# Folding two rows of a gate/up product in a matmul, fewer native down pieces and one more weight place

## The chip, the cores and the metric

The kernel runs on one core of one Trainium2 chip. The metric is the device time of one execution in microseconds (us); each timed value below is such an execution, and the median of them is compared. TensorE is called PE here, VectorE DVE, ScalarE ACT, GpSimd POOL and SyncE SP. Each engine runs its own instructions in the order in which the program's scheduler has put them; a weight load of PE (PEld) overlaps its matmuls.

## The reference

The program computes two blocks on 256 tokens of width 1024, all in float32. The first has adaptive normalisation, differential attention over 256 tokens and 256 context rows, a Fourier mixer, and a mixture of 32 experts of which each token takes two. The second has two layers of two feed-forward networks each, around a sparse attention and a gated mixer. What matters here is one expert:

```python
xb = h_pad[tok]                                          # rows of one expert
y = (jax.nn.silu(xb @ w_gate[e]) * (xb @ w_up[e])) @ w_down[e]
return y * wt[:, None]
```

`w_gate[e]` and `w_up[e]` are 1024 x 512, `w_down[e]` is 512 x 1024: 2 MiB each, 6 MiB an expert, 192 MiB for the 32 experts, all read from HBM once.

## The kernel before, in words

Weights stream in pieces of 1 MiB (128 partitions x 2048 float32). `load` (L59) issues the next piece on SP's queue into a place: five places belong to the pool `raw` (`RAW = 5`), and one more, `rawx`, is added from the end of the first block's mixer until the experts are done (`extend`, `NX = 1`). SP issues in stream order, and an issue waits until its place is free. For each expert the stream has four pieces of gate and up weights (g0, g1, u0, u1), and behind those of expert e the two down pieces of expert e-1 (d0, d1).

A split piece is cut into a high and a low part of the reduced float32 type that PE multiplies fastest: `split` (L151) rounds on ACT into `wh` (L152), and DVE subtracts into `wl` (L153). `ahead(3)` keeps up to three cut pieces in hand, in four buffers of each part; the place of a raw piece is free after its subtraction. A native piece is not cut: PE multiplies it as plain float32, and its place is free after those matmuls. `NATIVE` names (e mod 4, piece number); before, piece 5 (d1) is native in every expert.

One turn of the loop over e in `moe` does, in program order: `turn(e-1)`; the gate rows of e with g0 and g1 (`rows`); on every fourth e the one-hot selection of the next four experts (`hot`, DVE); two parts of `gather`; the up rows with u0 and u1; `place` (two transposes); `scatter(e-2)`; `down(e-1)` with d0 and d1. An expert has 64 places for tokens, and its stationary operand has 128 columns, 64 high parts and 64 low parts of the same tokens. So the product has two rows for each token, which must be added: `rows` copies the product from its PSUM bank to `gu0` or `gu1` (ACT, L1489), and `turn` transposes it on PE in four 128 x 128 pieces for gate and four for up (L1497); DVE adds the two rows in a reduction (`sum`, L1499). Then come silu (ACT, L1501), the product of gate and up (DVE, L1502) and its split into `act` (ACT and DVE, L152 and L153). `down` multiplies `act` with d0 and d1, and takes the result from PSUM scaled, as a high part on ACT (`yh`, L1520) and a low part on DVE (`yl`, L1521).

The order in which each engine does all this is laid down when the program is made, by a scheduler that puts ready instructions in by priority with durations of its own; so a piece's rounding on ACT can stand behind an instruction of another step that waits for PE, and then waits as well.

All matmuls go through `mm` (L143), so they have one line, L144; they are told apart by their tiles (moving operand first, then the stationary one).

Of the kernel before, what the change touches and what calls it, by code (L numbers as in the profile page):

```python
# [10 lines left out]
F32 = mybir.dt.float32  # L11
# [3 lines left out]
AF = mybir.ActivationFunctionType  # L15
OP = mybir.AluOpType
AX = mybir.AxisListType
PSUM = bass.MemoryType.PSUM
P = 128
# [1 line left out]
D = 1024  # L21
EPS = 1e-6
PIECE = 2048
RAW = 5
NX = 1
NEG = -1e30
SEL = -3e38
# [2 lines left out]
class Net:  # L30
    def __init__(self, ctx, tc, I, out):
        self.ctx, self.tc, self.nc, self.I, self.out = ctx, tc, tc.nc, I, out
        self.cp = self.pool(ctx, "const", 1)
        self.rawp = self.pool(ctx, "raw", RAW)
        self.psp = ctx.enter_context(tc.tile_pool(name="psum", bufs=4, space=PSUM))
# [8 lines left out]
        self.pieces = {}  # L44
        self.extra, self.extended, self.spare, self.slots_raw = {}, set(), 0, RAW
        self.parts = 1
# [43 lines left out]
    def extend(self, ctx, n):  # L90

        self.rawx = ctx.enter_context(self.tc.tile_pool(name="rawx", bufs=n, reuse_waits="tile", side="right"))
        self.spare, self.slots_raw = n, RAW + n
        self.run_loads()
# [1126 lines left out]
    def route_consts(self):  # L1221
        nc, I, cp = self.nc, self.I, self.cp
        self.idr = cp.tile([P, P], F32R, name="idr")
        nc.vector.tensor_copy(self.idr, self.idf)
        self.slots = cp.tile([P, P], F32, name="slots")
        nc.gpsimd.iota(self.slots, pattern=[[0, 2], [1, 64]], base=0, channel_multiplier=0,
                       allow_small_or_imprecise_dtypes=True)
        self.tri = cp.tile([P, P], F32, name="tri")
        nc.gpsimd.memset(self.tri, 1.0)
        nc.gpsimd.affine_select(out=self.tri, in_=self.tri, pattern=[[1, P]], compare_op=OP.is_gt, fill=0.0,  # L1230
                                base=0, channel_multiplier=-1)
        self.wr = cp.tile([P, 8, 36], F32, name="wr")
        nc.gpsimd.dma_start(self.wr[:, :, :4], I["w_router_group"][0].rearrange("(j p) e -> p j e", j=8))
        nc.gpsimd.dma_start(self.wr[:, :, 4:], I["w_router_expert"][0].rearrange("(j p) e -> p j e", j=8))
# [171 lines left out]
                            nc.vector.tensor_add(self.h[t][:, o], self.h[t][:, o], a)  # L1406


    NATIVE = ((0, 5), (1, 5), (2, 5), (3, 5))

    def native(self, e, n):

        return (e % 4, n) in self.NATIVE

# [15 lines left out]
    def moe(self):  # L1430
        nc, I = self.nc, self.I
        self.limit = self.moe_end
        with ExitStack() as ctx:
            mp = self.pool(ctx, "moe", 1)
            XG, G, GT, gu, act, ys, acc = {}, {}, {}, {}, {}, {}, {}
# [54 lines left out]
                gu[e, which] = sb  # L1490

            def turn(e):
                z = []
                for which in range(2):
                    ps = self.bank()
                    for a in range(4):
                        nc.tensor.transpose(ps[:, P * a : P * a + P], gu[e, which][:, P * a : P * a + P], self.idf)  # L1497
                    r = mp.tile([P, 4, 64], F32, name=f"sum{which}", bufs=1)
                    nc.vector.tensor_reduce(r, ps.rearrange("p (a i s) -> p a s i", a=4, i=2), axis=AX.X, op=OP.add)  # L1499
                    z.append(r)  # L1500
                nc.scalar.activation(z[0], z[0], AF.Silu)  # L1501
                nc.vector.tensor_mul(z[0], z[0], z[1])  # L1502
                A = mp.tile([P, 4, P], F32R, name="act", bufs=2)
                self.split(A[:, :, :64], A[:, :, 64:], z[0])
                act[e] = A

            def down(e):
# [33 lines left out]
            for e in range(34):  # L1541
                if e == 1:
                    self.parts = 1
                if 0 < e < 33:
                    turn(e - 1)
                if e < 32:
                    rows(e, 0)
                    if e % 4 == 0 and e < 28:
                        hot(e // 4 + 1)
                if e < 32:  # L1550
                    if e < 28:
                        for i in range(2):
                            gather(e // 4 + 1, 2 * (e % 4) + i)
                    rows(e, 1)
                    place(e)
                if e > 1:
                    scatter(e - 2)
                if 0 < e < 33:
                    down(e - 1)
# [105 lines left out]
```

## Time and profile before

| | before |
|---|---|
| median of 3 executions | 1911.88 us (1911.81 to 1913.43) |
| the profiled execution, own time | 1913.98 us |
| its span, first to last instruction | 1912.2 us |
| PE busy | 1837.8 us (96%) |
| DVE busy | 1327.7 us (69%) |
| ACT busy | 1146.4 us (60%) |
| POOL busy | 41.8 us (2%) |
| read from HBM | 447.92 MB, 235 GB/s over the span |

The experts take the stretch from about 226 to 800 us of the span. Busy time of PE is a union of modelled, pipelined matmuls: a PE that is busy all the time need not be at its peak. The DMA figure is the mean busy share of 16 DMA engines.

### The profile page before, as it was taken

What the parts mean: (1) busy time and instruction counts of PE and PEld (TensorE: products, weight loads), DVE (VectorE), ACT (ScalarE), POOL (GpSimd) and SP (SyncE); (2) the same over time, 40 slices, a digit from 0 to 9 for tenths busy, and PEclk for the clock granted to TensorE, in tenths of its full rate; (3) what the DMA queues carried; (4) which work ended last, traced back from release to release, by engine and by line L of the source; (5) the groups of instructions that cost most, each with busy time, mean ns of one, the idle gap of its engine ahead of it and who ended that gap; (6) DMA issues with size and microseconds to landing.
All of it is one profiled execution on the core that took longest, in us unless ns stands there. A gap on an engine that the chain in (4) does not pass through costs nothing.

```text
span 1912.2 us, 23030 instructions
## 1 busy us (share of the span) xinstructions
PE 1837.8 (96%) x8352; PEld 1439.9 (75%) x8352; DVE 1327.7 (69%) x2116; ACT 1146.4 (60%) x1924; POOL 41.8 (2%) x74
## 2 busy tenths in 40 slices
PE   6899699999999999999999999999999999999998
PEld 3677577766667666678888888887888888887886
DVE  2887788888888888865558765556555776765554
ACT  3555587778777777754456654446444755555443
POOL 2000000000000000000000000000000010100000
PEclk9999899999999999999999999999999999999999
DMA  9784398999999999865555455554555556665551
GB/s 301 257 284 144 111 340 356 349 357 353 351 357 352 353 365 367 277 220 177 179 179 178 155 176 198 198 186 153 190 198 198 182 172 198 199 218 191 181 180 43
DMA packets 189495, 450.51 MB, mean 236 GB/s; under 512 B 10170, under 2 KB 119066, under 8 KB 164802
## 3 DMA queue, kind: packets, MB, share of 16 engines
q1 hardware_dynamic: 185284, 437.26, 64.5%
q0 software_dynamic: 3808, 11.25, 2.1%
q8 instruction: 66, 1.08, 0.2%
q10 hardware_dynamic: 288, 0.52, 0.1%
q14 instruction: 49, 0.40, 0.1%
HBM read 447.92 MB, written 1.07 MB: 235 GB/s over the span
## 4 chain that ended last, share of the span: by engine, by line
PE 71%; DVE 8%; ACT 5%; issue 3%; DMA 1%; DVEq 0%; ACTq 0%; SPq 0%
PE bank_w L144 50%; PE bank_acc L144 17%; DVE wl L153 6%; ACT wh L152 3%; DMA raw<-w_up 1%; PE bank_w L1497 1%; PE bank_w L299 1%; ACT XG L1457 0%; PE bank_w L230 0%; ACT xh L233 0%; PE bank_w L702 0%; ACT L175 0%; DVE G L1440 0%; DVE yl L1521 0%; PE bank_w L490 0%
## 5 line engine op out<-in xcount | busy, mean ns | idle before, releaser
L153 DVE TENSOR_TENSOR wl<-raw,wh 128x512 fp32r<-128x512 f32 (+3 forms) x977 | 862.9, 936 | 301.4 <-ACT wh L152 299.0
L152 ACT CAST wh<-raw 128x512 fp32r<-128x512 f32 (+3 forms) x977 | 746.0, 823 | 285.2 <-PE bank_w L144 207.2
L144 PE MATMUL bank_w<-wh,xh 128*128 128x512 f32 (+2 forms) x1056 | 406.4, 385 | 4.1 <-ACT xh L233 3.4
L144 PE MATMUL bank_w<-wh,xl 128*128 128x512 f32 (+2 forms) x1056 | 402.7, 382 | 1.0 <-DVE xl L234 1.0
L144 PE MATMUL bank_w<-wl,xh 128*128 128x512 f32 (+2 forms) x1056 | 402.1, 381 | 0.0
L144 PEld LDWEIGHTS bank_w<-wh,xh 128*128 128x128 f32 x1056 | 199.0, 188 | 42.5 <-ACT xh L233 6.3
L144 PEld LDWEIGHTS bank_w<-wh,xl 128*128 128x128 f32 x1056 | 198.9, 188 | 38.0 <-DVE xl L234 2.5
L144 PEld LDWEIGHTS bank_w<-wl,xh 128*128 128x128 f32 x1056 | 199.0, 188 | 35.0 <-issue 0.2
L144 PE MATMUL bank_w<-wl,XG 128*128 128x512 f32 x512 | 208.7, 408 | 13.6 <-DVE wl L153 11.2
L144 PE MATMUL bank_w<-wh,XG 128*128 128x512 f32 x512 | 211.0, 412 | 0.1
L144 PE MATMUL bank_acc<-wh,th 128*128 128x512 f32 x352 | 144.2, 410 | 0.0
L144 PEld LDWEIGHTS bank_w<-wl,XG 128*128 128x128 f32 x512 | 96.0, 188 | 56.4 <-DVE wl L153 37.6
L144 PE MATMUL bank_acc<-wh,tl 128*128 128x512 f32 x352 | 137.7, 391 | 0.0
L144 PE MATMUL bank_acc<-wl,th 128*128 128x512 f32 x352 | 137.6, 391 | 0.0
L292 ACT ACTIVATE silu<-bank_w,rs 128x256 f32<-128x256 f32 x88 | 41.9, 476 | 155.4 <-PE bank_w L144 155.4
L294 DVE SCALAR_TENSOR_TENSOR hid<-bank_w,rs,silu 128x256 f32<-128x256 f32 x88 | 42.6, 484 | 116.7 <-ACT silu L292 113.3
L144 PEld LDWEIGHTS bank_w<-wh,XG 128*128 128x128 f32 x512 | 96.4, 188 | 23.2 <-issue 5.3
L144 PE MATMUL bank_w<-rawx,act 128*128 128x512 f32 x240 | 107.8, 592 | 0.0
L144 PEld LDWEIGHTS bank_w<-rawx,act 128*128 128x128 f32 x240 | 45.4, 189 | 45.5 <-issue 43.1
L144 PEld LDWEIGHTS bank_acc<-wh,tl 128*128 128x128 f32 x352 | 66.1, 188 | 14.1
L144 PEld LDWEIGHTS bank_acc<-wl,th 128*128 128x128 f32 x352 | 66.4, 189 | 11.2
L144 PEld LDWEIGHTS bank_acc<-wh,th 128*128 128x128 f32 x352 | 66.2, 188 | 11.1
(407 smaller groups left out, 2195.3 us busy)
## 6 DMA issues: line engine op xcount, KB each, us to landing
raw<-ffn_w_in SPq DMA_DIRECT2D x176, 512.0 KB, 4.7
raw<-w_up SPq DMA_DIRECT2D x64, 1024.0 KB, 7.9
raw<-w_gate SPq DMA_DIRECT2D x62, 1024.0 KB, 7.5
raw<-ffn_w_out SPq DMA_DIRECT2D x44, 1024.0 KB, 5.7
raw<-w_down SPq DMA_DIRECT2D x34, 1024.0 KB, 7.8
rawx<-w_down SPq DMA_DIRECT2D x30, 1024.0 KB, 6.4
raw<-w_ada SPq DMA_DIRECT2D x24, 1024.0 KB, 6.5
raw<-a_w_in SPq DMA_DIRECT2D x12, 1024.0 KB, 4.9
```

What stands on the lines that cost most here:

```text
L144: self.nc.tensor.matmul(*a, **k)
L152: self.nc.scalar.copy(h, src)
L153: self.nc.vector.tensor_sub(l, src, h.bitcast(F32))
L292: nc.scalar.activation(s, ps[:, :256], AF.Silu, scale=self.rs[t])
L294: nc.vector.scalar_tensor_tensor(hid[c, t], ps[:, 256:], self.rs[t], s, op0=OP.mult, op1=OP.mult)
L299: nc.tensor.transpose(ps[:, r, :], hid[c, t][:, P * r : P * r + P], self.idf)
L1497: nc.tensor.transpose(ps[:, P * a : P * a + P], gu[e, which][:, P * a : P * a + P], self.idf)
```

## The change

The fold matrix is a 128 x 64 constant of two 64 x 64 unit matrices, one below the other. In `turn` each 128 x 128 piece of `gu` becomes the stationary operand of a float32 matmul whose moving operand is the fold matrix (64 columns), so that the product is transposed and its two rows are added at once; gate and up share one PSUM bank. Silu and the product read that bank, and the two reductions and their two tiles go. `NATIVE` keeps one entry: d1 is native in 8 of the 32 experts (e mod 4 = 1), and in the other 24 it is split. `RAW` becomes 6, so that there are seven places with `rawx`. The reserve of SBUF in which POOL's DMA queue keeps its descriptors is set to 4096 bytes of a partition, where nothing was set before.

```diff
-RAW = 5
+RAW = 6
 ...
+        self.fold = cp.tile([P, 64], F32, name="fold")
+        nc.vector.tensor_add(self.fold, self.idf[:, :64], self.idf[:, 64:])
 ...
-    NATIVE = ((0, 5), (1, 5), (2, 5), (3, 5))
+    NATIVE = ((1, 5),)
 ...
             def turn(e):
-                z = []
+                ps = self.bank().rearrange("p (w a s) -> p w a s", w=2, a=4)
                 for which in range(2):
-                    ps = self.bank()
                     for a in range(4):
-                        nc.tensor.transpose(ps[:, P * a : P * a + P], gu[e, which][:, P * a : P * a + P], self.idf)
-                    r = mp.tile([P, 4, 64], F32, name=f"sum{which}", bufs=1)
-                    nc.vector.tensor_reduce(r, ps.rearrange("p (a i s) -> p a s i", a=4, i=2), axis=AX.X, op=OP.add)
-                    z.append(r)
-                nc.scalar.activation(z[0], z[0], AF.Silu)
-                nc.vector.tensor_mul(z[0], z[0], z[1])
+                        self.mm(ps[:, which, a, :], gu[e, which][:, P * a : P * a + P], self.fold, start=True, stop=True)
+                z = mp.tile([P, 4, 64], F32, name="z", bufs=1)
+                nc.scalar.activation(z, ps[:, 0], AF.Silu)
+                nc.vector.tensor_mul(z, z, ps[:, 1])
                 A = mp.tile([P, 4, P], F32R, name="act", bufs=2)
-                self.split(A[:, :, :64], A[:, :, 64:], z[0])
+                self.split(A[:, :, :64], A[:, :, 64:], z)
                 act[e] = A
 ...
-    nc = bacc.Bacc("TRN2", target_bir_lowering=False, num_devices=1)
+    nc = bacc.Bacc("TRN2", target_bir_lowering=False, num_devices=1, dynamic_dma_scratch_size=4096)
```

## Rows read from the trace of the kernel before

**Rows 1.** The page: DMA share in 40 slices (tenths), and POOL's queue (packets, MB, share).

```profile
DMA  9784398999999999865555455554555556665551
...
q0 software_dynamic: 3808, 11.25, 2.1%
```

**Rows 2.** Stretches: length, busy us (x instructions) by engine, PEclk, DMA share, GB/s.

```profile
428.34:499.69 71.35, 69.03 (x297) 49.37 (x297) 60.79 (x47) 53.77 (x56) 0.00 (x0) 1.00 0.95 355
278.39:326.93 48.54, 48.53 (x219) 36.58 (x219) 38.08 (x33) 36.05 (x39) 0.00 (x0) 1.00 0.90 364
712.54:782.16 69.62, 66.34 (x266) 45.02 (x265) 58.87 (x45) 50.24 (x48) 0.00 (x0) 1.00 0.95 366
...
297.00:309.00 12.00, 12.00 (x54) 9.05 (x53) 8.81 (x5) 8.56 (x11) 0.00 (x0) 1.00 1.01 424
...
850.00:900.00 50.00, 50.00 (x226) 41.20 (x226) 26.56 (x49) 23.60 (x48) 0.00 (x0) 1.00 0.56 189
```

**Rows 3.** The chain that ended last, one expert: start us, us, what.

```profile
571.05 4.83 PE bank_w L144 x14
576.49 1.91 ACT wh L152
578.43 2.30 DVE wl L153
...
583.03 2.29 DVE wl L153
585.36 2.34 PE bank_w L144 x9
587.70 0.87 PE bank_w L1497 x8
588.58 4.83 PE bank_w L144 x14
```

**Rows 4.** Timeline of one expert: start, us, engine, what [idle before <-releaser].

```profile
503.38 2.29 DVE L153 TENSOR_TENSOR wl<-raw,wh 128x2048 fp32r<-128x2048 f32 x1 [1.38 <-ACT wh L152]
...
504.55 0.69 ACT L1520 ACTIVATE yh<-bank_w,gslot 128x512 fp32r<-128x512 f32 x1 [0.61 <-PE bank_w L144]
...
507.07 6.87 DVE L153 TENSOR_TENSOR wl<-raw,wh 128x2048 fp32r<-128x2048 f32 x3
...
515.90 0.59 ACT L1489 COPY gu<-bank_w 128x512 f32<-128x512 f32 x1 [1.72 <-PE bank_w L144]
```

**Rows 5.** Groups by shape, 285 to 785 us: count | busy us, mean ns | idle before.

```profile
L153 DVE TENSOR_TENSOR wl<-raw,wh 128x2048 fp32r<-128x2048 f32 x140 | 319.6, 2291 | 50.1 <-ACT wh L152 48.3
L152 ACT CAST wh<-raw 128x2048 fp32r<-128x2048 f32 x141 | 269.5, 1917 | 2.6 <-DMA raw<-w_gate 1.7 <-PE bank_w L144 0.9
...
L1499 DVE TENSOR_REDUCE sum<-bank_w 128x256 f32<-128x512 f32 x58 | 37.6, 686 | 10.8 <-PE bank_w L1497 10.8
...
L1502 DVE TENSOR_TENSOR sum<-sum,sum 128x256 f32<-128x256 f32 x29 | 12.3, 425 | 2.9 <-DVE sum L1499 0.5
```

**Rows 6.** Groups of PE by shape, the whole span.

```profile
L1497 PE MATMUL bank_w<-idf,gu 128*128 128x128 f32 x256 | 33.4, 273 | 0.9 <-ACT gu L1489 0.9
...
L144 PE MATMUL bank_acc<-v,aT 128*128 128x128 f32 x64 | 8.4, 276 | 0.0
...
L144 PE MATMUL bank_w<-wr,xaT 128*128 128x36 f32 x32 | 4.1, 274 | 0.7 <-ACT xaT L1250 0.7
```

**Rows 7.** Timeline of PE: the first matmul of d0, and d1.

```profile
304.45 0.39 PE L144 MATMUL bank_w<-wh,act 128*128 128x512 f32 x1
...
306.26 3.59 PE L144 MATMUL bank_w<-rawx,act 128*128 128x512 f32 x8
```

**Rows 8.** Waits of SP's queue, 285 to 785 us: total, times, longest.

```profile
SPq L71 <- PE bank_w L144: 152.0, 28, 8.3
```

**Rows 9.** The chain that ended last, start and end of the experts.

```profile
265.38 7.97 DMA raw<-w_up
...
761.55 8.27 DMA raw<-w_up
```

## The prediction

> **What bounds the kernel now.** I read the page first, for where the work of the change lies: the DMA share stands at eight tenths or more through the slices of the experts and falls to about five behind them [rows 1]. In a feed-forward stretch behind them PE is busy 50.00 of 50 us while the DMA engines are busy 0.56 [rows 2], so a weight that lands earlier is worth nothing there, and the gain or loss has to come from the experts, some 575 us.
>
> Second, the stretches. Four consecutive experts in the middle take 71.35 us, or 17.84 each. In that time PE is busy 69.03, DVE 60.79 and ACT 53.77 us, 15.2 and 13.4 an expert. Three early experts take 48.54 us, 16.18 each, with PE busy all of it: 16.2 is about PE's own load for one expert. The last ones take 69.62 for four, 17.4 each [rows 2].
>
> Third, the chain of waits, for why an expert in the middle takes 17.5 and not 16.2. It goes round once an expert, from 571.05 to 588.58, that is 17.53: 4.83 us of PE, of which the last part is the native down piece; then ACT, whose next rounding (576.49) starts when the results of that product have been taken out; three subtractions of DVE back to back (578.43 to about 585.3, with PE's products beside them); then PE with u1 and the eight transposes [rows 3]. The timeline shows the same order from ACT and DVE: the second `yh` waits 0.61 us for PE, and three subtractions take 6.87 us behind one rounding [rows 4]. So no engine is full. The native piece is in this chain with its whole length, and the d1 of three experts in four is what the change shortens on PE.
>
> Fourth, SP's queue. In 500 us it stands 28 times, 152.0 us together, behind a load that waits for PE [rows 8]: the place `rawx` is given back only when the native product is done, and the loads of the next gate pieces are queued behind it. Yet the DMA engines aren't the limit: with loads queued they moved 424 GB/s for 12 us on end, where the middle runs at 355 [rows 2].
>
> **The change part by part.** *Native to split, on PE.* The eight records of a native d1 take 3.59 us; the eight of d0, which is split and has the same shape, take 306.26 - 304.45 = 1.81 [rows 7]. In 24 experts PE is relieved of 1.78 us.
>
> *The fold, on PE.* Eight transposes go: 33.4 us for 256 of them is 0.130 each, 1.04 for eight [rows 6]. Eight float32 matmuls come, and each is two records, as the router's 16 matmuls with `wr` are 32 records. With 36 moving columns a record took 4.1 / 32 = 0.128 us, with 128 columns 8.4 / 64 = 0.131 [rows 6]; 64 columns lie between, so 16 x 0.13 = 2.08, or 1.04 more, in all 32 experts. The ends: 0, if a matmul of this size were one record, and 16 x 0.276 = 4.4 us, 3.4 more, if none overlapped the next (276 ns is the length of one [rows 6]). I take 1.04, since all three rows show the overlap.
>
> These records are paced by the load of the stationary operand, since 36 and 128 columns cost the same. The Trainium skill, page "TensorE: Matmul & The Clock Gate", section "LDWEIGHTS (loading the stationary operand)", gives the number of columns over 1.2 in ns, about 107 ns for 128. By it 16 records would be an estimated 1.7 us, 0.67 more than now, and the time some 11 us lower than forecast; the rows show 0.128 to 0.131, so I stay with them.
>
> *Sums, on DVE.* Two reductions of 686 ns go [rows 5], 1.37 us an expert. They are not on the chain; what they give is room. Silu and the product keep their size, and now read a bank: no more than the reduction, which reads twice as many elements from one, so the product's 425 ns [rows 5] may rise to 0.69 at most. I take no change; the end is 0.26 on each of two engines.
>
> *The added splits.* 24 times 1917 ns on ACT and 2291 ns on DVE [rows 5]. DVE's load in such an expert becomes 15.2 - 1.37 + 2.29 = 16.1 us, ACT's 13.4 + 1.92 = 15.3, PE's 16.18 - 1.78 + 1.04 = 15.4. In a native expert they are 13.8, 13.4 and 17.2. What has to hide the new split is the room in which the two engines now wait, DVE 1.38 us behind a rounding and ACT 1.72 for PE before a copy [rows 4], with the 1.37 of the sums. If they find it, the chain of a split expert is 17.53 - 1.78 + 1.04 = 16.79; that is above all three loads, but DVE is close, and is what is late next. A native expert goes to 17.53 + 1.04 = 18.57. The selection, once in four, stays: 71.35 - 3 x 17.53 = 18.76, 1.23 more than an ordinary one. Four experts: 3 x 16.79 + 18.57 + 1.23 = 70.17, or 1.18 less than 71.35. From 326.93 to 712.54 there are 385.6 / 17.84 = 21.6 experts, 5.4 fours: 6.4 us less.
>
> *One more place.* Where the chain goes through a load that was issued only when a place came free, the place takes it off. That is so at the start (7.97 us at 265.38) and again among the last experts (8.27 at 761.55) [rows 9]. At the start one MiB more lies ready: 1.05 MB at 424 GB/s is 2.5 us. Among the last four, at 17.4 each though they have no gather left, I take 0.75 each, 3 us, which is what the shorter chain would give. The early three experts are PE's own: two of them lose 0.74 us and one gains 1.04, so 0.4 less. In the rest of the program a place gives 0; the lower end there is where PE is not always busy, before 250 us, and I leave 2 us either way for a new order of instructions.
>
> *The smaller reserve for POOL's queue.* That queue took 2.1% of the DMA engines' time [rows 1], and none of the chain's waits above is for it. I take 0, with up to 5 us of loss if a transfer now waits for descriptors.
>
> Sum: -6.4 - 2.5 - 3 - 0.4 = -12.3 us, from the profiled execution's own 1913.98 (a span of 1912.2 and 1.8 around it). That execution was 2.1 above the median of the runs, 1911.88, from which I count: 1911.88 - 12.3, about 1899.
>
> **The rivals.** *A, slower: the new split joins the chain.* ACT does its instructions in order. If the rounding of d1 stands behind the copy of `gu`, which waits for u1 on PE [rows 4], DVE can't start the new subtraction in its room. Then the round is DVE's load except the d0 subtraction that it does meanwhile, and PE's u1, the copy and the rounding in a row: 16.1 - 2.29 + 1.81 + 0.59 + 1.92 = 18.1 us, 0.6 more than now, with 1.04 in the native expert: 2.8 for four experts, 20 us over seven fours; less the 2.5 of the start, about 1929. It decides when more than 0.74 us of the split stays on the chain. For it speaks that ACT waits there now, against it the room and the earlier landing of d1. Chance 0.22.
>
> *B, much faster: PE's load is the limit.* If splits are ready early as in the early three experts, four take 3 x 15.4 + 17.2 = 63.4 and the selection is hidden: 7.95 less, 43 us over 5.4 fours, with 5 at the end and 2.5 at the start: about 1862. SP's queue, free of 24 of 32 waits for PE, speaks for it; that DVE and ACT at 16.1 and 15.3 are then as full as PE speaks against. Chance 0.16.
>
> *C, the transfers are the limit.* If HBM gave no more over whole experts than about what the middle draws, each would stay near 17.6: 6.29 MB at 358 GB/s is 17.57, so 0.27 less than 17.84 over 21.6 experts, 6 us, with the start 1903. The 12 us at 424 GB/s speak against it. The Trainium skill, page "DMA: Bandwidth & Descriptors", section "Where 436 GB/s comes from", states a limit of about 358 GB/s for a core on HBM transfers, which would be this case; the row shows more than that. Chance 0.06.
>
> *D, given back.* The new split takes 0.4 of the 0.74 gained, and three such experts pay for one native one: the middle is as before, and the start's 2.5 is left, 1909. Chance 0.18.
>
> **How the numbers follow.** The forecast has 0.38; its own range is 1887 to 1909 (a fold at the page's price, or half the room found). This kernel's time can be told from no change by about 0.2%, 3.8 us. Faster: nearly all of the forecast, B and C, and a third of D: 0.36 + 0.16 + 0.05 + 0.05 = 0.62. Same: the rest of D and of the forecast, 0.15. Slower: A and what POOL's reserve could cost, 0.23. The range leaves out the lower part of B and the upper of A, about a tenth each: 1870 to 1926.
>
> **What would show it.** In the profile after: 16 records of the fold in about 2.1 us; no reductions at that line; 24 more roundings and subtractions; SP's waits for PE down to about a quarter in count. An expert with a split d1 at 16.8 us from chain to chain and one with a native d1 at 18.6, four in 70.2. Wrong would be: a wait of DVE for the rounding of d1 behind the copy of `gu` (A), PE busy without gaps at 16 us an expert (B), DMA share at 1.0 throughout with ACT waiting for landings (C), or time moved outside the experts.

## The result, and the profile after

The changed kernel takes 1935.25 us (median of 4, 1931.92 to 1937.38), the kernel before 1912.66 beside it. The ratio is 1.0115, with a 95% interval of 1.0097 to 1.0132: slower by 1.2%, where 1899 was forecast. The profiled execution has a span of 1930.2 us, 18.0 more than before.

Stretches of the changed kernel come first, in the columns of [rows 2]: four experts in the middle, three early ones, and the feed-forward stretch.

```profile
479.91:553.60 73.69, 68.67 (x328) 53.00 (x328) 61.16 (x41) 59.16 (x60) 0.00 (x0) 1.00 0.92 343
267.63:315.02 47.39, 47.39 (x240) 38.81 (x240) 42.32 (x30) 40.03 (x43) 0.00 (x0) 1.00 0.98 394
850.00:900.00 50.00, 50.00 (x228) 41.23 (x227) 26.56 (x48) 23.45 (x48) 0.00 (x0) 1.00 0.58 190
```

Four experts take 73.69 us in place of 71.35 [rows 2]. The early three are still PE's, a little shorter than before, and the feed-forward stretch is as it was. In the middle PE is busy 68.67 us and DVE 61.16, hardly different, and ACT 59.16, 5.4 more for three roundings: no engine is full, and the four take longer all the same.

The chain of waits through one expert with a split d1 shows where (start, us, what; steps of "issue" under 0.05 us are left out here and below):

```profile
502.00 1.91 ACT wh L152
503.93 2.31 DVE wl L153
506.28 0.99 PE bank_w L144 x3
507.30 0.69 ACT yh L1520
...
517.68 2.30 DVE wl L153
520.02 1.91 ACT wh L152
521.96 2.30 DVE wl L153
```

From 503.93 to 521.96 is one round, 18.03 us. In [rows 3] a round is one long piece of PE, one rounding and three subtractions. Here it goes from ACT to DVE for d1 alone, for less than a microsecond to PE, and back to ACT: it is mostly ACT and DVE.

The timeline says what they wait for; ACT, then DVE, then PE in the same stretch, with the idle time before an instruction and its releaser in brackets.

```profile
519.54 0.59 ACT L1491 COPY gu<-bank_w 128x512 f32<-128x512 f32 x1 [1.89 <-PE bank_w L144]
520.02 1.90 ACT L152 CAST wh<-raw 128x2048 fp32r<-128x2048 f32 x1
```

```profile
513.06 6.92 DVE L153 TENSOR_TENSOR wl<-raw,wh 128x2048 fp32r<-128x2048 f32 x3
521.96 2.29 DVE L153 TENSOR_TENSOR wl<-raw,wh 128x2048 fp32r<-128x2048 f32 x1 [1.99 <-ACT wh L152]
```

```profile
519.80 1.89 PE L144 MATMUL bank_w<-fold,gu 128*128 128x64 f32 x16
524.31 0.50 PE L144 MATMUL bank_w<-wl,act 128*128 128x512 f32 x1 [0.71 <-DVE wl L153]
```

ACT stands 1.89 us for PE before it copies the up rows (519.54), and the rounding of d1 is behind that copy (520.02). DVE finished its three subtractions at 519.98 and stands 1.99 us until that rounding is done. The wait of ACT before the copy is hardly longer than before (1.72 in [rows 4]); what is new is that DVE's next work is queued behind it. The chain puts the rounding at 520.02 behind DVE's subtraction of d0, which ended 0.04 us earlier. That is not what it waits for: in e10 below the rounding of d1 follows that of d0 at once, and DVE is still at d0. PE then stands for DVE in the middle of the down product (524.31).

Of SP's queue, 285 to 785 us (total, times, longest), the row that answers to [rows 8]:

```profile
SPq L71 <- PE bank_w L144: 18.5, 3, 6.2
```

28 waits of 152.0 us became 3 of 18.5, fewer still than the quarter that was forecast, and no time came of it.

For the tables below I take from each trace the start of the first transpose or fold matmul of every turn; the distance of two is the time of an expert. Before, three are 17.53 and the fourth, with the selection, 18.77. After, three with a split d1 are 17.99; the fourth, which has the native d1 and the selection, is 19.69, and among the last experts, where no selection falls, the native one is 18.45. The 18.0 us of the span are: 11.3 in the five fours of the middle, 2.6 in the last four experts, 5.4 behind the last turn, and -1.2 ahead of these (rounded).

### The profile page after: what moved, and what is told of

It is laid out like the page before. It is cut to its first block, busy times and chain, and to the rows that moved or that the text cites. A ratio compares the mean times of both kernels' runs of the same rounds, so it can differ in the third digit from the quotient of the medians.

```text
span 1930.2 us, 23566 instructions
## 1 busy us (share of the span) xinstructions
PE 1840.0 (95%) x8608; PEld 1471.3 (76%) x8608; DVE 1334.8 (69%) x2077; ACT 1188.9 (62%) x1948; POOL 41.9 (2%) x74
## 3 DMA queue, kind: packets, MB, share of 16 engines
q0 software_dynamic: 3808, 11.25, 2.0%
## 4 chain that ended last, share of the span: by engine, by line
PE 64%; ACT 10%; DVE 9%; issue 5%; DMA 0%; DVEq 0%; ACTq 0%
PE bank_w L144 46%; PE bank_acc L144 16%; DVE wl L153 7%; ACT wh L152 7%; PE bank_w L299 1%; ACT yh L1520 1%; ACT XG L1459 1%; PE bank_w L230 0%; ACT xh L233 0%; DMA raw<-ffn_w_out 0%; PE bank_w L702 0%; DVE G L1442 0%; ACT L175 0%; ACT junk L160 0%; ACT GT L1467 0%
## 5 line engine op out<-in xcount | busy, mean ns | idle before, releaser
L144 PE MATMUL bank_w<-wh,XG 128*128 128x512 f32 x512 | 204.2, 399 | 0.0
L144 PE MATMUL bank_w<-wl,act 128*128 128x512 f32 x224 | 85.8, 418 | 13.5 <-DVE wl L153 13.5
L144 PE MATMUL bank_w<-wh,act 128*128 128x512 f32 x224 | 81.0, 396 | 2.4 <-DVE act L153 2.4
L1491 ACT COPY gu<-bank_w 128x512 f32<-128x512 f32 x64 | 38.1, 595 | 60.6 <-PE bank_w L144 60.6
```

The lines of the kernel that those rows point to most:

```text
L144: self.nc.tensor.matmul(*a, **k)
L1491: nc.scalar.copy(sb.rearrange("s (a p) -> s a p", a=4), ps.rearrange("s (p a) -> s a p", a=4))
```

## The experiments

Theory 1 is rival A of the prediction: time is set by a round of waits through ACT's fixed order, whatever the loads. Theory 2: the engines' loads set it, so that the added work itself is the price. Theory 3: the place or POOL's smaller reserve does. Every time is a median beside runs of the kernel before, with the ratio to it.

**The parts alone.** The first takes the fold and leaves every d1 native; the second takes the splits alone; the third has the place and the reserve alone; the fourth leaves these two out.

```diff
 # e1, from the changed kernel
-RAW = 6
+RAW = 5
-    NATIVE = ((1, 5),)
+    NATIVE = ((0, 5), (1, 5), (2, 5), (3, 5))
-num_devices=1, dynamic_dma_scratch_size=4096)
+num_devices=1)
 # e2, from the kernel before
-    NATIVE = ((0, 5), (1, 5), (2, 5), (3, 5))
+    NATIVE = ((1, 5),)
 # e3, from the kernel before
-RAW = 5
+RAW = 6
-num_devices=1)
+num_devices=1, dynamic_dma_scratch_size=4096)
 # e4, from the changed kernel
-RAW = 6
+RAW = 5
-num_devices=1, dynamic_dma_scratch_size=4096)
+num_devices=1)
```

> Only the fold: d1 native in all experts, five places and one, POOL's reserve untouched. Theory 1 (the round of waits through ACT's fixed order): the fold lies on that round with its whole length, and the reductions that go do not; 16 records took 1.89 us in the changed kernel where eight transposes took 1.04, so 0.85 more an expert, some 24 to 27 us over 28 to 32 experts: 1936 to 1940. Theory 2 (the engines' loads set the time): DVE is relieved of 1.37 us an expert and PE stays under 17.1, so no slower than before: 1905 to 1914.

> Only the added splits: d1 split in 24 experts, transposes and reductions as before, five places and one. Theory 1: ACT has the rounding of d1 behind the copy of gu as in the changed kernel, DVE stands 2 us and then does 16.0 + 1.37 us: about 19.3 an expert with a split d1 against 17.5, so 24 x 1.8 = 43 more: 1945 to 1960. Theory 2: DVE's load becomes 17.5 and the round is just that: 1912 to 1920.

> Only the place and POOL's smaller reserve. Theory 1: the middle does not wait for landings, so only the start and the last experts gain, 2 to 5 us: 1907 to 1911. Rival (theory 3): the place or the reserve is what made the changed kernel slower: 1920 or more.

> The changed kernel without the place and with POOL's reserve untouched. Theory 1: 1935 to 1940, as the changed kernel or a few us above. Theory 3: back at 1912 to 1920.

| run | median us | ratio, 95% interval | an expert, us |
|---|---|---|---|
| e1, the fold | 1943.15 | 1.0164 (1.0140 to 1.0188) | 18.44, with the selection 19.68 |
| e2, the splits | 1931.27 | 1.0088 (1.0063 to 1.0113) | 17.99, native with the selection 18.78 |
| e3, place and reserve | 1913.28 | 0.9996 (0.9986 to 1.0007) | |
| e4, fold and splits | 1936.75 | 1.0124 (1.0102 to 1.0146) | |

Theory 3 is out: the place and the reserve do nothing by themselves (e3, where theory 1 had 2 to 5 us of gain), and leaving them out changes nothing (e4). The two were only run together, so a gain of one and a cost of the other that cancel are not excluded. The fold alone costs more than the whole change, 3 us more than theory 1 allowed: an expert takes 0.91 us more, which is the fold's longer stay on PE. In its chain PE's piece is 8.95 us, where the three pieces of [rows 3] from 585.36 on make 8.04; then ACT, DVE and PE follow as before:

```profile
528.42 8.95 PE bank_w L144 x39
537.40 0.02 ACT yh L1520
...
537.98 1.91 ACT wh L152
539.92 2.30 DVE wl L153
```

Theory 2 fails there: DVE has less to do and the kernel is slower by 29 us. For e2 both missed, theory 1 by 14 us too much and theory 2 by 11 too little. Its DVE shows why it is no slower than the changed kernel in a split expert, though it has the reductions:

```profile
525.65 1.29 DVE L1499 TENSOR_REDUCE sum<-bank_w 128x256 f32<-128x512 f32 x2 [0.46 <-PE bank_w L1497]
527.18 2.29 DVE L153 TENSOR_TENSOR wl<-rawx,wh 128x2048 fp32r<-128x2048 f32 x1 [0.24 <-ACT wh L152]
```

The two reductions stand in the place in which the changed kernel's DVE stands still before d1 (521.96 above). So in the changed kernel the 1.37 us that the fold takes off DVE come out as waiting: 17.99 us with them or without.

**The order on ACT, one edge at a time.** The four kernels that follow have the instructions of the changed kernel, or of the kernel before, and another order on ACT. `issue_after` queues an instruction behind another of the same engine and adds no wait for its end; `cuts` lists the roundings of weight pieces as they are written.

```diff
 # ahead(): each rounding of a weight piece is kept
+            self.cuts.append(self.rounded)
 # yh (e5, e7, e8): behind the rounding of the second next gate piece
+                    with self.tc.issue_after(self.cuts[-2]):
                         nc.scalar.activation(yh, ps[half], AF.Copy, scale=gs)
 # the copy of the up rows (e6, e7), where d1 is split: behind the rounding of d1
+                    with self.tc.issue_after(self.cuts[-2]):
                         nc.scalar.copy(sb.rearrange("s (a p) -> s a p", a=4), ps.rearrange("s (p a) -> s a p", a=4))
```

> The changed kernel with one order: on ACT the taking out of the down product (yh) comes behind the rounding of the second next gate piece, not ahead of it. The same instructions otherwise. Theory 1: the product of d1 and its yh leave the round, the rounding starts 1.5 us earlier in each expert: about 16.5 for a split expert in place of 18.0, some 40 us less, 1885 to 1905. Theory 2 (loads): the instructions are the same, so the time stays: 1931 to 1939.

> The changed kernel with another order: where d1 is split, the copy of the up rows (gu) on ACT comes behind the rounding of d1, not ahead of it. Theory 1: DVE's 2 us without work between d0 and d1 go, and up to 1.2 us of an expert with them, 24 to 30 us: 1903 to 1915; less if the scheduler, given this, moves the rounding of act further back. Theory 2: 1931 to 1939.

> The changed kernel with both orders. Theory 1: at or below the better of the two, 1875 to 1900. Theory 2: 1931 to 1939.

> The kernel before with yh behind the rounding of the second next gate piece. Theory 1: the native product and its yh leave the round of 17.5 us, which then is PE's load or DVE's, 16.2 to 16.8: 1880 to 1895, the better version of all. Theory 2: 1909 to 1915.

| run | median us | ratio, 95% interval |
|---|---|---|
| e5, after, yh behind | 1951.14 | 1.0191 (1.0173 to 1.0209) |
| e6, after, copy behind | 1925.74 | 1.0063 (1.0045 to 1.0081) |
| e7, after, both | 1918.57 | 1.0026 (1.0015 to 1.0038) |
| e8, before, yh behind | 1947.63 | 1.0178 (1.0159 to 1.0196) |

Theory 2 can't stand: the same instructions take from 1918.57 to 1951.14. But theory 1 had the sign wrong in two of four (e5, e8), and in the other two forecast far more than came: 1903 to 1915 for e6 and 1875 to 1900 for e7. In e5 and e8 the scheduler, given one edge, had moved something else. ACT of e5:

```profile
501.93 0.59 ACT L1493 COPY gu<-bank_w 128x512 f32<-128x512 f32 x1 [1.03 <-PE bank_w L146]
502.41 1.90 ACT L154 CAST wh<-raw 128x2048 fp32r<-128x2048 f32 x1
```

Now the copy of the gate rows (501.93) stands ahead of the rounding of the last up piece (502.41) and waits for PE: the same fault in another place. These two runs say nothing on yh itself.

e6 is the plain test of the wait shown above. It is gone: DVE takes d0, d1 and the next piece on end. But a split expert still takes 17.65, only 0.34 less, and its chain now goes through `yh`, behind which ACT rounds the second gate piece of the next expert (DVE, then the chain):

```profile
517.24 6.70 DVE L155 TENSOR_TENSOR wl<-raw,wh 128x2048 fp32r<-128x2048 f32 x3 [0.26 <-ACT wh L154]
```

```profile
517.03 6.68 PE bank_w L146 x36
523.73 0.69 ACT yh L1526
...
525.01 1.91 ACT wh L154
```

So the rounding of d1 behind the copy is one place of several in which ACT's order holds an expert up. (In e6 the scheduler also put the rounding of `act` later, as its expectation feared, and half of the fold behind the product of d0.) With yh behind as well, e7, a split expert takes 17.25.

**The order held in all places.** So that little but the intended move is left, the copy of the gate rows is kept behind the rounding of the last up piece, where it is in both kernels.

```diff
 # both copies of rows; e9, e11, e12: "not which" alone
+                if 1 < e < 31 and (not which or not self.native(e - 1, 5)):
+                    with self.tc.issue_after(self.cuts[-2]):
                         nc.scalar.copy(*copy)
 # yh behind, as above, in all four; e12 has RAW = 6 and the reserve of 4096 as well
```

> The kernel before with two orders on ACT: yh behind the rounding of the second next gate piece, as in the run before on this kernel, and the copy of the gate rows kept behind the rounding of the last up piece, where it was in the kernel before and from which the scheduler had moved it in that run. Theory 1: the native product leaves the round, an expert takes PE's load or DVE's, 16.2 to 16.9: 1880 to 1897. Rival (theory 4): the later yh itself costs, since the down product's two PSUM banks are held longer: 1920 or more, as in that run.

> The changed kernel with the gate rows' copy kept behind the rounding of the last up piece, the up rows' copy behind the rounding of d1, and yh behind the rounding of the second next gate piece. Theory 1: DVE is without gaps at 16.1 and the round is 16.3 to 17.0 for a split expert: 1885 to 1905. Theory 2 (loads): 1931 to 1939. Theory 4: above 1918.

> The fold alone (d1 native everywhere, five places and one) with the two orders of the run on the kernel before. Theory 1: the fold is then on PE's load alone, 16.2 + 0.85 = 17.0 an expert: 1900 to 1912, and 0.85 x 28 = 24 us more than the kernel before with the same orders if that one is bound by PE, less if it is bound by DVE. Theory 4: as without the orders, 1940 or more.

> The kernel before with the two orders, the sixth place and POOL's smaller reserve. Theory 1: with the round shorter, SP's wait for the native product's place starts to count, and one more place covers it: 2 to 10 us below the same without the place. Rival: no difference, the place is worth nothing while rawx blocks SP's queue.

| run | median us | ratio, 95% interval | an expert, us |
|---|---|---|---|
| e9, before | 1911.64 | 0.9994 (0.9984 to 1.0003) | 17.61, with the selection 17.80 |
| e10, after | 1899.80 | 0.9923 (0.9907 to 0.9940) | 16.57, native with the selection 18.14 |
| e11, the fold | 1921.90 | 1.0039 (1.0025 to 1.0054) | |
| e12, before with place | 1910.80 | 0.9989 (0.9978 to 1.0001) | |

e10 settles that the order is the cause: the changed kernel, with the same instructions and added edges on ACT alone, is 35 us quicker and 0.8% under the kernel before. The scheduler laid out PE and DVE a little otherwise too: half of the fold, for instance, stands behind the product of d0. The stretch of four experts, then ACT and DVE around d1:

```profile
485.96:553.79 67.83, 66.30 (x328) 53.10 (x328) 60.58 (x42) 58.27 (x60) 0.00 (x0) 1.00 0.97 375
```

```profile
517.31 3.76 ACT L154 CAST wh<-raw 128x2048 fp32r<-128x2048 f32 x2
521.01 0.59 ACT L1496 COPY gu<-bank_w 128x512 f32<-128x512 f32 x1
521.50 1.91 ACT L154 CAST wh<-raw 128x2048 fp32r<-128x2048 f32 x1
```

```profile
519.29 6.70 DVE L155 TENSOR_TENSOR wl<-raw,wh 128x2048 fp32r<-128x2048 f32 x3 [0.25 <-ACT wh L154]
```

The busy times are those of the changed kernel to a microsecond or two (60.58 and 61.16 for DVE), and the four take 67.83 us in place of 73.69. Two roundings run without a gap (517.31, d0 and d1), the copy behind them waits for nothing, and DVE's subtractions of d0, d1 and the next piece run on end.

The cleanest pair is e7 and e10. Over 18 experts of the middle PE and DVE do the same operations in the same order in both, and on ACT two neighbours are exchanged in each expert, the copy of the gate rows and the rounding of the last up piece. ACT of e7, then of e10:

```profile
506.79 0.59 ACT L1497 COPY gu<-bank_w 128x512 f32<-128x512 f32 x1 [0.57 <-PE bank_w L146]
507.28 1.91 ACT L154 CAST wh<-raw 128x2048 fp32r<-128x2048 f32 x1
```

```profile
514.29 1.93 ACT L154 CAST wh<-raw 128x2048 fp32r<-128x2048 f32 x1
516.10 0.60 ACT L1496 COPY gu<-bank_w 128x512 f32<-128x512 f32 x1
```

That takes a split expert from 17.25 to 16.57, a native one with the selection from 19.53 to 18.14, and the kernel from 1918.57 to 1899.80: an exchange on an engine that is busy 58.27 of 67.83 us.

e9 is a miss for theory 1 as I had put it: the native product and yh were taken off the round, and nothing came of it. Its chain had gone over to the turn:

```profile
511.81 0.45 PE bank_w L1504 x4
512.28 1.30 DVE sum L1506 x2
...
514.44 1.90 ACT wh L154
516.37 2.30 DVE wl L155
518.72 2.14 PE bank_w L146 x8
```

Transposes, reductions, silu and the rounding of `act`, and only behind that, on ACT, the next piece's rounding (514.44): a second round of 17.6 us. So the kernel before is likely to have had two rounds of nearly the same length.

e11 is a miss too, 1921.90 where theory 1 had 1900 to 1912: PE is busy 17.87 of the 17.89 us of an ordinary expert there, and not 17.0. In e12 the place with the reserve gives less than 1 us on e9, where theory 1 had 2 to 10.

**What was still open.** Which round holds the kernel before, whether the fold pays once there are splits, whether the place has a part, and what holds the native experts. For e13 and e16 silu in the turn is queued behind the rounding of the next first gate piece:

```diff
 # e13 (from e9) and e16 (from e10)
+                    with self.tc.issue_after(self.cuts[-3]):
                         nc.scalar.activation(z[0], z[0], AF.Silu)      # z, ps[:, 0] in e16
 # e14: the orders of e10 on e2; e15: e10 with RAW = 5 and no reserve set
```

> The kernel before with three orders on ACT: the two of the last run on it, and silu of the turn behind the rounding of the next first gate piece. In the run with two, the chain went through the turn (reductions, silu, the rounding of act, and only then the next rounding), 17.6 us as before. Theory 1: with this the turn leaves the round as well, and PE's load or DVE's is left, 16.2 to 17.0 an expert: 1880 to 1900. Theory 5 (the kernel before is held by something else than ACT's order): 1907 to 1915 again.

> The added splits with the transposes and reductions, five places and one, and the orders that brought the changed kernel to 1900. Theory 1: the round is DVE's load, 15.2 + 2.29 = 17.5 for a split expert, so the orders help little here: 1912 to 1928, and the reductions' 1.37 us that the fold takes away are what makes the changed kernel with the orders quicker than this. Rival: the fold gives nothing, 1896 to 1904 as with it.

> The changed kernel with the orders, with five places and one and POOL's reserve untouched. Theory 1: at 16.6 us an expert (6.29 MB, 380 GB/s) the native product of one expert in four blocks SP for less than a piece, so 0 to 5 us more than with the place: 1899 to 1905. Rival: the place is what lets the orders work, 1912 or more.

> The changed kernel with the orders and silu behind the rounding of the next first gate piece in the native experts too. Theory 1: the native expert (18.1 with the selection in the run with the orders) loses its wait of 1.65 us at silu, some 1 us in 8 experts: 1888 to 1897. Rival: PE has 17.2 us of work there, so nothing changes: 1897 to 1902.

| run | median us | ratio, 95% interval | four experts, us |
|---|---|---|---|
| e13, before, three orders | 1891.07 | 0.9872 (0.9856 to 0.9889) | 67.6 |
| e14, splits with e10's orders | 1918.09 | 1.0020 (1.0011 to 1.0030) | 69.9 |
| e15, e10 without the place | 1899.91 | 0.9926 (0.9910 to 0.9943) | 67.9 |
| e16, after, three orders | 1896.79 | 0.9906 (0.9889 to 0.9922) | 67.6 |

All four came into the range of theory 1, e16 only just: its 1896.79 touches the rival's 1897, and a native expert with the selection lost 0.3 us (18.14 to 17.83) and not 1. What holds the native experts is not shown. e13 is the quickest of all kernels run here, 1.3% under the kernel before, and has none of the change. Two experts of four there have a chain that is PE's almost from end to end:

```profile
523.80 7.51 PE bank_w L146 x27
531.31 0.91 PE bank_acc L146 x4
532.22 2.29 PE bank_w L146 x12
534.51 0.13 PE bank_w L1464 x2
534.63 1.00 PE bank_acc L146 x4
535.63 3.88 PE bank_w L146 x17
539.51 0.88 PE bank_w L1504 x8
540.39 7.47 PE bank_w L146 x27
```

From 523.80 to 540.39 is one expert, 16.59 us, without a step to another engine. So taking away both rounds does what taking away one did not; silu's order without yh's was not run. In e14 a split expert is 17.36, of which DVE is busy 16.7 and PE 16.0; with the fold it is 16.57 (e15). So the fold does pay 0.8 us where splits make DVE the fullest engine, and costs 0.9 where PE is in the round. The place is worth nothing in this order either: e15 and e10 are 0.1 us apart.

## Why the prediction was wrong

**What bounds the kernel.** Right in that no engine was full, and that the experts decide most of it (11.3 and 2.6 of the 18.0 us, as split up above). Incomplete: the chain shows the one round that ended last, and a second of the same length, through the turn, was not seen until e9 took the first away.

**The step that failed** is "If they find it, the chain of a split expert is 17.53 - 1.78 + 1.04 = 16.79", the room for the added split. Idle time of ACT and DVE was counted as room for the new split. But ACT does its work in a fixed order, and what stood ahead of a rounding there waited for PE: the rounding of d1 stood behind the copy of the up rows, DVE stood 1.99 us, and the expert took 17.99. Without that one place it took 17.65 (e6), without the one behind yh 17.25 (e7), and without the exchange that came of it 16.57 (e10). Over four experts 73.66 was measured (3 x 17.99 + 19.69) where 70.17 was forecast; of these 3.5 us the split experts are 3 x 1.20. With the order mended the same instructions gave 1899.8 us (e10), against 1899 forecast. That the totals agree is luck: four experts took 67.83 and not 70.17, the place below gave nothing, and the stretch behind the last turn was 6.9 us longer than before.

**Rival A** named that place, "behind the copy of `gu`", and said 1929. It came within 6 us, with 18.1 us for a split expert (17.99) and 1.04 more for a native one (0.92). I had given it 0.22, because I weighed how much room there was, and not in what order ACT would come to it. That order is fixed when the program is made. The closeness is in part luck: e6 shows that a second round of 17.65 lay just under the one that it names.

**The fold on PE.** The term was 1.04 more than the transposes, and e1 measured 0.91 an expert. The prices of both were read too high. A group's busy time runs to the end of its last matmul, which overlaps what follows; PE is held up only to the start of the next one. The transposes before, and the fold in the changed kernel, each with the matmul behind it (start, us):

```profile
516.16 1.04 PE L1497 MATMUL bank_w<-idf,gu 128*128 128x128 f32 x8
516.95 0.47 PE L144 MATMUL bank_w<-wl,act 128*128 128x512 f32 x1
```

```profile
519.80 1.89 PE L144 MATMUL bank_w<-fold,gu 128*128 128x64 f32 x16
521.51 0.48 PE L144 MATMUL bank_w<-wl,act 128*128 128x512 f32 x1
```

From start to start that is 0.79 and 1.71, so 0.92 more, against the 0.91 of e1. In an expert with a native d1 it lies on the round in full, as forecast (18.45 against 18.57). The Trainium skill, page "TensorE: Matmul & The Clock Gate", section "LDWEIGHTS (loading the stationary operand)", leads to an estimated 1.7 us for the sixteen. The trace agrees with that, with 1.71; the prediction set it against the 1.04 of the transposes, and so had 0.67 by it.

**The reductions** were called room and no gain. Right, and more so than meant: alone, the fold made the kernel slower by 29 us (e1).

**One more place** was put at 5.5 us, 2.5 at the start and 3 among the last experts. Together with the reserve it gave nothing by itself (e3), with the order (e15 against e10), or on the kernel before with the order (e12 against e9). In e3 the landings at 265 and 761 us are no longer in the chain, and the time is the same: what took their place was as late. **POOL's reserve** was taken at 0; no run has it without the place, and the two together cost nothing (e3).

**Rivals B to D.** B needed PE to be the limit; with the orders the split experts come near it (16.57), as the changed kernel stands they don't. C is out: four experts of e10 draw 375 GB/s, more than the 358 of that rival. D had the middle as before, and it was 2.3 us longer for four experts.

The 5.4 us behind the last turn come with the splits: in all ten kernels that have them this stretch is 3.0 to 6.9 us longer than before, and in the others from 0.3 shorter to 2.2 longer. How is not shown. There the chain of the changed kernel has a landing of 6.46 us for the first feed-forward network, but no run takes it by itself.

## What to carry to other kernels

Where in-order engines feed each other, an added instruction can cost what it is queued behind, not its length: before pricing it against idle time, find out which instruction will stand ahead of it on its engine, and what that one waits for. Check for a second chain of about the same length before crediting the removal of the first. And when only an order is tested, look at the whole order that came out: one fixed pair can move another instruction into the same fault.

## What the runs showed of the hardware that was not expected

In rows of float32 matmuls with a 128 x 128 stationary operand, the records follow each other at 0.112 us (median from start to start) with 64 moving columns, and at 0.112 with 36 and with 128 [rows 6]: at these sizes the moving columns don't show in the time. Busy time over count gave 0.128 and 0.131 there, because the last matmul of each short row counts in full. Setting POOL's descriptor reserve to 4096 bytes did not show in the time of a program with 11.25 MB on that queue (0.9996, 0.9986 to 1.0007, with the sixth place).
